# Eight of a layer's sixteen mixer gates made by a seven-product scheme at the mixer's front; FFN slices of 6, 8 and 8

## The chip, the cores and the metric

One core of one Trainium2 chip runs the whole decoder trunk in one launch. The time is the device time of one execution in microseconds, the median of several runs. All times inside an execution are microseconds from the start of its profiled span.

## The reference

Two layers over 512 tokens with 1024 channels, in float32. Only what the change touches is shown.

```python
for l in range(DEPTH):                                   # DEPTH = 2
    x = x + 0.5 * swiglu(rms_norm(x, ffn1_norm[l]), ffn1_w_up[l], ffn1_w_down[l])
    h = rms_norm(x, mix_norm[l])
    proj = h @ w_in[l]
    q, k, v, z, xbc, dt_raw, gate_sb, gate_ssm = jnp.split(proj, IN_SPLITS, axis=-1)
    y_sb  = stick_breaking_attention(q, k, v) @ w_branch_sb[l]        # 4 heads x 128
    y_ssm = mamba2_mixer(z, xbc, dt_raw, ...) @ w_branch_ssm[l]       # 24 heads x 64, 8 groups, state 128
    merged = jax.nn.sigmoid(gate_sb) * y_sb + jax.nn.sigmoid(gate_ssm) * y_ssm
    x = x + merged @ w_out[l]
    x = x + 0.5 * swiglu(rms_norm(x, ffn2_norm[l]), ffn2_w_up[l], ffn2_w_down[l])
return rms_norm(x, final_norm)
```

The two gates of a layer are 1024 channels each, so 8 blocks of 128 for each: sixteen gate blocks a layer. The hidden width of a feed-forward network (FFN) is 2816, or 22 blocks.

## The kernel before

Everything is held transposed, channels on the 128 partitions and the 512 tokens along the free axis; x is eight tiles of 128 x 512. A float32 product is made of three passes: weight and input are split into a high part (fp32r) and a low part, and `mm3` (lines 360 to 364) adds high x high, low x high and high x low. The weights come from one DRAM array, `wflat`, in units, in the order of `unit_order`. A plain unit is eight 128 x 128 blocks (512 KB): `fetch` loads it, `convert` makes its high part on ScalarE (line 327) and its low part on VectorE (line 329) two units ahead of its use. `dense` multiplies it, three matmuls of 512 columns a block.

A product X W with both sides cut in halves (tokens in two, input channels in two, output columns in two) needs eight products of halves. For pairs of FFN blocks (gate and up of blocks j and j+1) `pair_of_blocks` makes it from seven, named `SEVEN`: "11", "12", "s2", "s1", "s3", "s4", "22". Four use weights as stored, three use sums of weights (made by accumulating DMAs on GpSimd's queue, `onto`, line 289, or by VectorE, `add`, line 303). Three of the factors are differences of the input's halves, which `combine` makes (two ScalarE and four VectorE steps, then the split, lines 420 to 440) while the last products of the part before run. A product is 2 x 4 blocks of three matmuls of 256 columns.

The inputs h are x times the norm's gain; the root mean square `rs` is known only later (`norm_end`), so what is made before is scaled by `rs` afterwards. At the head of a seven-product FFN the pairs 0 and 2 come first as `leading`: "11" and "12" of both, which need no differences, then the rest.

A layer runs FFN 1, the mixer, FFN 2. An FFN runs in slices of its 22 blocks: gate and up of the slice's blocks, then eight `down` products over the slice. The slices are 8, 8 and 6 blocks, in FFN 2 of layer 0 they are 6, 8 and 8. The first six blocks of the first FFN are plain units.

The mixer (line 1376): first q, k, v and the attention; then the steps of `group_steps`: for each of four pairs p of state-space groups one z (four units), two b, two c and three x blocks, with gate units (`gs`, `gm`) put between them; then two `bsb` units (attention's branch product, four blocks each), then, for each of eight output blocks, the two `bssm` units (twelve blocks) with further `bsb` units between, and at last the `out` units. Twelve gates (`EARLY` = 6, times two) are squashed by a tanh (line 1351) and kept in DRAM (`gd`) until the merge, four stay in SBUF. In pair 0 there are four gate units, in pairs 1, 2 and 3 there are three, two and one, then two more, then the last four.

What is not a matmul of `dense` is written as generators that are advanced by `tick()`, once after each block of a unit (`by_tokens`, which makes z, ticks 24 times). A `yield n` waits n ticks. So the order of all instructions on each engine is fixed when the program is written, and the chip's engines run it in that order with semaphores between them. `conv_block` is the convolution behind each x, b and c unit, ending in transposes on TensorE that wait in `meet` for a common moment. `ssd_group` is one group: it starts when its inputs are there and the group before has ended, issues the matmuls of its first two and then of its last two chunks (lines 1243 and 1246), normalises (lines 1310 to 1320), and transposes the result (line 914) for `bssm`. `flush()` ticks until no generator is left, without matmuls of units; it stands behind the two `bsb` units.

Queues: SP issues the weight loads, the spills of gates and of x; GpSimd's queue the accumulating loads.

Of the kernel before, what the change touches and what calls it, by code (L numbers as in the profile page):

```python
# [12 lines left out]
ALU = mybir.AluOpType  # L13
# [38 lines left out]
G_D = G_ALOG + HEADS  # L52
NPAR = G_D + HEADS
EARLY = 6
MERGE_ORDER = tuple(range(EARLY, KB)) + tuple(range(EARLY))
OUT_ORDER = tuple(i // 2 + KB // 2 * (i % 2) for i in range(KB))
TAPS = KCONV + 1
# [3 lines left out]
def group_steps():  # L61

    gates = iter([(t, m) for m in range(EARLY) for t in ("gs", "gm")])
    for p in range(GROUPS // 2):
        a, b = 2 * p, 2 * p + 1
        if p == 0:
            steps = [("z", p), ("b", a), 1, ("c", a), ("x", 0), 1, ("x", 1), ("x", 2), 1, ("b", b), ("c", b), 1]
        else:  # L70
            steps = [("b", a), ("c", a), p < 2, ("x", 3 * p), ("x", 3 * p + 1), 1, ("z", p), ("x", 3 * p + 2),
                     ("b", b), p < 3, ("c", b), 0]
        for step in steps:
            if step in (0, 1):
                if step:
                    yield next(gates)
            else:
                yield step
    yield from gates
    for m in range(EARLY, KB):  # L80
        yield "gs", m
        yield "gm", m
# [20 lines left out]
def qkv_order():  # L103


    for h in range(SBH):
        yield from (("q", h), ("k", h))
        if h == SBH - 2:
            for u in range(NT):
                yield "v", u  # L110


def slices(layer, f):

    return ((0, 6), (6, 14), (14, 22)) if (layer, f) == (0, 2) else ((0, 8), (8, 16), (16, 22))


def pairs_from(layer, f):

    return {(0, 1): 6}.get((layer, f), 0)  # L120


def leading(layer, f):

    return [(layer, f, "pair", j, part) for j, parts in
            ((0, SEVEN[:2]), (2, SEVEN[:2]), (0, SEVEN[2:]), (2, SEVEN[2:])) for part in parts]


def unit_order(layer):

    def ffn(f):
        for s, (j0, j1) in enumerate(slices(layer, f)):
            start = j0
            if s == 0 and not pairs_from(layer, f):
                for key in leading(layer, f):
                    yield key, KB
                j0 = 4
            for j in range(j0, j1):
                if j < pairs_from(layer, f):
                    yield (layer, f, "gate", j), KB  # L140
                    yield (layer, f, "up", j), KB
                elif j % 2 == 0:
                    for part in SEVEN:
                        yield (layer, f, "pair", j, part), KB
            for m in OUT_ORDER:
                yield (layer, f, "down", s, m), j1 - start

    yield from ffn(1)
    for t, h in qkv_order():
        yield (layer, t, h), KB  # L150
    for kind, i in group_steps():
        if kind == "z":
            for u in range(NT):
                yield (layer, "z", i, u), 2 * 2 * GW // P + (i == 0)
        else:
            yield (layer, kind, i), KB
    for m in MERGE_ORDER[:2]:
        yield (layer, "bsb", m), SBH
    for i, m in enumerate(MERGE_ORDER):
        yield (layer, "bssm", m, 0), 6  # L160
        yield (layer, "bssm", m, 1), 6
        if i + 2 < KB:
            yield (layer, "bsb", MERGE_ORDER[i + 2]), SBH
    for m in OUT_ORDER:
        yield (layer, "out", m), KB
    yield from ffn(2)
# [12 lines left out]
class Builder:  # L179
# [433 lines left out]
        yield 2  # L613
        yield from self.split(parts, a)

    def pair_of_blocks(self, base, fp, two):

        nc, half, n = self.nc, SEQ // 2, KB // 2  # L620
        a, b = slice(0, half), slice(half, SEQ)
        diff = self.diff
        chain, ps2 = (self.t(self.pmm, [P, SEQ], "mm") for _ in range(2))
        ps3 = self.t(self.pa, [P, SEQ], "pa")

        def product(ps, part, rhs, cols, start):
            hi, lo = self.unit(*base, part)
            for j in range(2):
                for k in range(n):
                    ks = slice((j * n + k) * P, (j * n + k + 1) * P)  # L630
                    self.mm3(ps[:, j * half:(j + 1) * half], (hi[:, ks], lo[:, ks]),
                             [r[:, cols] for r in rhs[k]], start and j + k == 0, k == n - 1, skip_group_check=True)
                    if k % 2:
                        self.tick()

        def activate(g, c, cols):

            while self.rs is None:
                yield 1
            norm(nc.gpsimd if c is up1 and not lead else nc.vector, g, cols)  # L640
            yield (5 + 2 * base[-1] if lead else 4) if c is up1 else 1
            self.tables(False)
            nc.scalar.activation(g, g, AF.Silu)
            yield 1
            if c is up1:
                norm(nc.vector if lead else nc.gpsimd, g, cols)
                yield 1 if lead else 3
            while not c:
                yield 1
            r = self.t(fp, [P, SEQ], "a")  # L650
            nc.vector.scalar_tensor_tensor(r, c[0], -1.0, g, op0=ALU.mult, op1=ALU.mult)
            yield 1
            r = r.rearrange("p (j t) -> p j t", j=2)
            yield from self.split([t.rearrange("p (j t) -> p j t", j=2)[:, :, cols] for t in two], r)

        def normed_up(c):
            while self.rs is None:
                yield 1
            norm(nc.gpsimd, c, b)
            yield 3  # L660
            up2.append(c)

        def norm(eng, r, cols):
            r = r.rearrange("p (j t) -> p j t", j=2)
            eng.tensor_tensor(r, r, self.rs[:, cols].unsqueeze(1).to_broadcast([P, 2, half]), op=ALU.mult)  # L665

        up1, up2 = [], []
        lead = not pairs_from(*base[:2]) and base[-1] < 4
        g1, g2 = (self.t(fp, [P, SEQ], "g", bufs=4) for _ in range(2))
        product(chain, "11", self.h[:n], a, True)  # L670
        nc.scalar.copy(g1, chain)
        product(ps2, "12", self.h[n:], a, True)
        nc.vector.tensor_tensor(g1, g1, ps2, op=ALU.add)  # L673
        self.spawn(activate(g1, up1, a))
        yield
        while None in self.diff:
            self.tick()
        product(chain, "s2", diff[n:], b, False)
        nc.scalar.copy(g2, chain)
        product(ps3, "s1", diff[:n], a, True)  # L680
        c = self.t(fp, [P, SEQ], "c", bufs=2)
        nc.scalar.copy(c, ps3)
        product(chain, "s3", diff[:n], b, False)
        nc.vector.tensor_tensor(c, chain, c, op=ALU.add)
        self.spawn(normed_up(c))
        product(ps3, "s4", self.h[n:], b, False)
        nc.vector.tensor_tensor(g2, g2, ps3, op=ALU.add)
        self.spawn(activate(g2, up2, b))
        product(chain, "22", diff[n:], a, False)
        up1.append(chain)  # L690

    def down(self, pd, m, gain, last):
        x = self.x[m]
# [98 lines left out]
    def ffn(self, layer, f, gain, gain_next):  # L792
        tc = self.tc
        with tc.tile_pool(name=f"act{layer}{f}", bufs=8, reuse_waits="tile") as ap, \
                tc.tile_pool(name=f"ffn{layer}{f}", bufs=3, reuse_waits="tile") as fp:
            self.gated = {}
            for s, (j0, j1) in enumerate(slices(layer, f)):
# [41 lines left out]
                for i, m in enumerate(OUT_ORDER):  # L839
# [11 lines left out]
                    if last and i == 0:  # L851
                        self.norm_start()
                        self.xd = self.t(self.dr, [KB, P, SEQ], "xd") if f == 1 else None
                        if f == 1:
                            self.close_t()
                    self.spawn(self.down(ps, m, gain_next, last))


# [517 lines left out]
    def mixer(self, layer):  # L1376
        nc, tc = self.nc, self.tc
        self.y_sb, self.y_ssm = [], [None] * (DIN // P)
        gain = self.pars[layer][:, G_MIX:G_MIX + KB]
        self.open_norm(self.x, gain)  # L1380
        self.hx = []
        first = []
        order = list(qkv_order())
        for i in range(4):
            while i == 3 and self.scaled_blocks < KB // 2:
                self.tick()
            first.append(self.project(layer, *order[i], swap=i == 3, aside=i < 2))
        xd, self.xd = self.xd, None
        self.xpool.__exit__(None, None, None)
        with ExitStack() as mix:  # L1390
            enter = mix.enter_context
# [4 lines left out]
                tc.tile_pool(name=f"yt{layer}", bufs=24, side="right", reuse_waits="tile"))  # L1396
            gp = enter(tc.tile_pool(name=f"gates{layer}", bufs=2, reuse_waits="tile"))
            gates, self.gated = {}, {}

            self.gd = self.t(self.dr, [2 * EARLY, P, SEQ], "gd")  # L1400

            def open_gate(t, m):
                ps, _ = self.project(layer, t, m)
# [136 lines left out]
def lay_out(inputs):  # L1540
# [6 lines left out]
    for layer in range(DEPTH):  # L1547
# [2 lines left out]
        dt_w = np.zeros((DM, 64), np.float32)  # L1550
        dt_w[:, :HEADS] = w_in[:, OFF_DT:OFF_DT + HEADS]
        for key, n in unit_order(layer):
            kind = key[1] if key[1] not in (1, 2) else key[2]
            if kind == "pair":
                if key[-1] not in STORED:
                    continue
                r0, c0 = {"11": (0, 0), "12": (DM // 2, 0), "s1": (0, FFN), "22": (DM // 2, FFN)}[key[-1]]
                c0 += key[3] * P
                w = a[f"ffn{key[1]}_w_up"][layer][r0:r0 + DM // 2]
                blk = np.concatenate([w[:, c0:c0 + P], w[:, c0 + P:c0 + 2 * P]])  # L1560
            elif kind in ("gate", "up"):
                w = a[f"ffn{key[1]}_w_up"][layer]
# [76 lines left out]
```

## Time and profile before

| | us |
|---|---|
| median of 3 runs | 2551.49 (2551.28 to 2551.67) |
| profiled execution | 2551.46 |
| its span | 2549.7 |
| TensorE busy | 2539.5 |
| VectorE busy | 1731.6 |
| ScalarE busy | 1282.3 |
| GpSimd busy | 533.5 |

TensorE's busy time is the union of its instructions' intervals, whose ends are modelled, so it says that the queue never ran dry, not that the array was at its peak. How long one matmul holds the array is read from start to start of successive matmuls. In layer 0 the mixer's first projections start at about 350 us, the first group of the state-space part at 512, the merge at about 811; FFN 2 begins at about 942, FFN 1 of layer 1 at about 1274.

### The profile page before, as it was taken

Reading aid. Unit: us, or ns where it says so; the run is one execution under the profiler, and the core shown is the slowest. Engines: PE = TensorE matmul, PEld = TensorE weight load, DVE = VectorE, ACT = ScalarE, POOL = GpSimd, SP = SyncE. Lnnn points to the kernel's source line nnn. Section 1 sums busy time; section 2 is a strip of 40 time slices with the busy share of each in tenths; the row PEclk is TensorE's granted clock in tenths of the full one; section 3 lists DMA queues with packets and bytes.
Section 4 is the critical chain, followed back from the end, with each engine's and each line's share of the span. In section 5 each row is a group of like instructions: output and inputs, shape, how many; then the busy total and the mean of one; then the engine's idle time right before and its main releaser. Section 6 shows DMA issues by size and latency. Waiting matters only on the chain.

```text
span 2549.7 us, 38576 instructions
## 1 busy us (share of the span) xinstructions
PE 2539.5 (100%) x15248; PEld 2287.1 (90%) x15248; DVE 1731.6 (68%) x2240; ACT 1282.3 (50%) x2121; POOL 533.5 (21%) x642
## 2 busy tenths in 40 slices
PE   9999999999999999999999999999999999999998
PEld 8898988888898889989898989888988888999997
DVE  8576875666664477758895858756666644876766
ACT  6343556655554264435563535566655633643434
POOL 0131301043342001313121312011433310122220
PEclk9999999999999999999999999999999999999999
DMA  6454542232333475646564545323333335746562
GB/s 192 133 153 145 135 138 80 96 120 97 113 111 102 137 211 150 174 149 165 181 159 141 158 141 143 130 80 108 113 97 104 115 111 160 197 139 172 145 164 83
DMA packets 107684, 346.80 MB, mean 136 GB/s; under 512 B 12208, under 2 KB 15728, under 8 KB 107504
## 3 DMA queue, kind: packets, MB, share of 16 engines
q1 hardware_dynamic: 93536, 295.98, 35.1%
q0 software_dynamic: 13104, 47.72, 10.5%
q8 instruction: 120, 1.97, 0.3%
q10 hardware_dynamic: 864, 0.64, 0.1%
q14 instruction: 60, 0.49, 0.1%
HBM read 331.61 MB, written 12.68 MB: 135 GB/s over the span
## 4 chain that ended last, share of the span: by engine, by line
PE 98%; DVE 1%; issue 1%; DMA 0%; ACT 0%; POOL 0%; DVEq 0%; SPq 0%; POOLq 0%; ACTq 0%
PE mm L362 27%; PE mm L364 27%; PE mm L363 27%; PE pa L363 3%; PE pa L362 3%; PE pa L364 3%; PE pa L1243 2%; PE pa L1246 1%; PE pt L1225 1%; PE pt L914 1%; PE pt L1221 1%; DMA s<-in_wflat_dram 0%; PE pa L501 0%; PE pa L914 0%; PE pa L1031 0%
## 5 line engine op out<-in xcount | busy, mean ns | idle before, releaser
L327 ACT CAST whi<-wraw 128x1024 fp32r<-128x1024 f32 (+3 forms) x437 | 432.3, 989 | 692.4 <-PE mm L364 495.3
L329 DVE TENSOR_TENSOR wlo<-wraw,whi 128x1024 fp32r<-128x1024 f32 (+3 forms) x437 | 535.9, 1227 | 272.3 <-ACT whi L327 271.5
L362 PE MATMUL mm<-hhi,whi 128*128 128x512 f32 (+1 forms) x1536 | 533.5, 347 | 0.0
L364 PE MATMUL mm<-hlo,whi 128*128 128x512 f32 (+1 forms) x1536 | 526.8, 343 | 0.0
L363 PE MATMUL mm<-hhi,wlo 128*128 128x512 f32 (+1 forms) x1536 | 526.3, 343 | 0.0
L364 PEld LDWEIGHTS mm<-hlo,whi 128*128 128x128 f32 x1536 | 288.0, 187 | 35.4
L363 PEld LDWEIGHTS mm<-hhi,wlo 128*128 128x128 f32 x1536 | 288.6, 188 | 32.3
L362 PEld LDWEIGHTS mm<-hhi,whi 128*128 128x128 f32 x1536 | 288.5, 188 | 31.9
L362 PE MATMUL mm<-th,whi 128*128 128x256 f32 x984 | 275.4, 280 | 0.0
L363 PE MATMUL mm<-th,wlo 128*128 128x256 f32 x984 | 274.7, 279 | 0.5 <-DVE wlo L329 0.5
L364 PE MATMUL mm<-tl,whi 128*128 128x256 f32 x984 | 274.5, 279 | 0.0
L362 PE MATMUL mm<-act,whi 128*128 128x512 f32 (+1 forms) x710 | 273.9, 386 | 0.0
L363 PE MATMUL mm<-act,wlo 128*128 128x512 f32 (+1 forms) x710 | 273.7, 386 | 0.0
L364 PE MATMUL mm<-act,whi 128*128 128x512 f32 (+1 forms) x710 | 273.7, 385 | 0.0
L329 DVE TENSOR_TENSOR wlo<-s,whi 128x1024 fp32r<-128x1024 f32 x164 | 237.6, 1462 | 34.6 <-ACT whi L327 31.3
L665 POOL TENSOR_TENSOR g<-g,rs 128x512 f32<-128x512 f32 x70 | 148.9, 2127 | 506.9 <-DVE g L673 475.7
L289 POOL DMA_DIRECT2D s<-in_wflat_dram x91 | 79.7, 890 | 624.2 <-DMA s<-in_wflat_dram 509.9
L327 ACT CAST whi<-s 128x1024 fp32r<-128x1024 f32 x164 | 172.0, 1049 | 67.8 <-PE mm L364 48.8
L694 DVE SCALAR_TENSOR_TENSOR x<-mm,x 128x512 f32<-128x512 f32 x93 | 64.2, 690 | 206.6 <-PE mm L364 206.6
L364 PEld LDWEIGHTS mm<-tl,whi 128*128 128x128 f32 x984 | 184.9, 188 | 0.0
L362 PEld LDWEIGHTS mm<-th,whi 128*128 128x128 f32 x984 | 184.7, 188 | 0.2 <-issue 0.2
L363 PEld LDWEIGHTS mm<-th,wlo 128*128 128x128 f32 x984 | 184.1, 187 | 0.7 <-DVE wlo L329 0.7
(305 smaller groups left out, 5110.0 us busy)
## 6 DMA issues: line engine op xcount, KB each, us to landing
wraw<-in_wflat_dram SPq DMA_DIRECT2D x325, 512.0 KB, 3.7
s<-in_wflat_dram POOLq DMA_DIRECT2D x91, 512.0 KB, 7.4
s<-in_wflat_dram SPq DMA_DIRECT2D x85, 512.0 KB, 5.2
wraw<-in_wflat_dram SPq DMA_DIRECT2D x88, 384.0 KB, 3.1
cumb<-cum_d SPq DMA_DIRECT2D x16, 768.0 KB, 5.0
xd<-x SPq DMA_DIRECT2D x16, 256.0 KB, 2.4
wraw<-in_wflat_dram SPq DMA_DIRECT2D x16, 256.0 KB, 3.8
x<-xd SPq DMA_DIRECT2D x16, 256.0 KB, 5.5
```

What stands on the lines that cost most here:

```text
L289: self.nc.gpsimd.dma_start(raw, self.stored(key[:-1] + (part,)), accum_op=ALU.add)
L327: nc.scalar.copy(hi[:, :n], raw[:, :n])
L329: nc.vector.tensor_tensor(lo[:, :n], raw[:, :n], hi[:, :n].bitcast(F32), op=ALU.subtract)
L362: mm(ps, a[0], b[0], start=start, stop=False, **kw)
L363: mm(ps, a[1], b[0], start=False, stop=False, **kw)
L364: mm(ps, a[0], b[1], start=False, stop=stop, **kw)
L665: eng.tensor_tensor(r, r, self.rs[:, cols].unsqueeze(1).to_broadcast([P, 2, half]), op=ALU.mult)
L694: self.nc.vector.scalar_tensor_tensor(x, pd, 0.5, x, op0=ALU.mult, op1=ALU.add)
L914: self.nc.tensor.transpose(pt[:, cs], src[:, cs], self.ident)
L1221: nc.tensor.matmul(cb, bt[:, span(c)], ct[:, span(c)], start=True, stop=True)
L1225: nc.tensor.matmul(pu, btok[:, c, :], xws[c].rearrange("p h d -> p (h d)"), start=True, stop=True)
L1243: nc.tensor.matmul(near[:, at:at + HD], decs[c][:, i, :], xdts[c][:, i, :], start=True, stop=True)
```

## The change

Eight of the sixteen gates of a layer, blocks 2 to 5 of both kinds, leave `group_steps` and are made at the mixer's head, ahead of q, as two fours (block m and m+1 of both gates) of seven products each. `four_gates` takes the four results as they come, scales them by `rs` on VectorE, squashes them on ScalarE and writes each as two half blocks of 128 KB to `gd`. `pair_of_blocks` is cut in two: `seven` holds the products, and what becomes of the results is handed in. The differences of the input's halves are now made at the end of FFN 1 too, since the pool that holds them (`tpool`) stays open until the fours are done. Of the gate units among the group steps only the four of pair 0 and the last four stay. The slices are 6, 8 and 8 in all FFNs but the last, which keeps 8, 8 and 6.

```diff
+FRONT = 2
...
-    gates = iter([(t, m) for m in range(EARLY) for t in ("gs", "gm")])
+    gates = iter([(t, m) for m in range(FRONT) for t in ("gs", "gm")])
     for p in range(GROUPS // 2):
         a, b = 2 * p, 2 * p + 1
         if p == 0:
             steps = [("z", p), ("b", a), 1, ("c", a), ("x", 0), 1, ("x", 1), ("x", 2), 1, ("b", b), ("c", b), 1]
         else:
-            steps = [("b", a), ("c", a), p < 2, ("x", 3 * p), ("x", 3 * p + 1), 1, ("z", p), ("x", 3 * p + 2),
-                     ("b", b), p < 3, ("c", b), 0]
+            steps = [("b", a), ("c", a), ("x", 3 * p), ("x", 3 * p + 1), ("z", p), ("x", 3 * p + 2), ("b", b), ("c", b)]
...
-    yield from gates
     for m in range(EARLY, KB):
         yield "gs", m
         yield "gm", m
...
-    return ((0, 6), (6, 14), (14, 22)) if (layer, f) == (0, 2) else ((0, 8), (8, 16), (16, 22))
+    return ((0, 8), (8, 16), (16, 22)) if (layer, f) == (DEPTH - 1, 2) else ((0, 6), (6, 14), (14, 22))
...
     yield from ffn(1)
+    for key in leading(layer, 0):
+        yield key, KB
...
+    def normed_half(self, eng, out, r, cols):
+        r, out = (t.rearrange("p (j t) -> p j t", j=2) for t in (r, out))
+        eng.tensor_tensor(out, r, self.rs[:, cols].unsqueeze(1).to_broadcast([P, 2, SEQ // 2]), op=ALU.mult)
...
+    def four_gates(self, base, m, fp):
+        nc, half = self.nc, SEQ // 2
+        a, b = slice(0, half), slice(half, SEQ)
+        def squash(src, t, cols, scale):
+            while self.rs is None:
+                yield 1
+            r = self.t(fp, [P, SEQ], "c", bufs=2) if t and cols is a else src
+            self.normed_half(nc.vector, r, src, cols)
+            yield 2
+            self.tables(False)
+            nc.scalar.activation(r, r, AF.Tanh, scale=scale)
+            yield 4
+            for j in range(2):
+                nc.sync.dma_start(self.gd[2 * (m + j) + t][:, cols], r[:, j * half:(j + 1) * half])
+        def take(*how):
+            return lambda src: self.spawn(squash(src, *how))
+        return self.seven(base, fp, take(0, a, 0.5), take(1, b, -0.5), take(0, b, 0.5), take(1, a, -0.5))
...
                         self.norm_start()
                         self.xd = self.t(self.dr, [KB, P, SEQ], "xd") if f == 1 else None
-                        if f == 1:
-                            self.close_t()
...
         gain = self.pars[layer][:, G_MIX:G_MIX + KB]
+        self.gd = self.t(self.dr, [2 * EARLY, P, SEQ], "gd")
+        front = ExitStack()
+        fp = front.enter_context(tc.tile_pool(name=f"front{layer}", bufs=2, reuse_waits="tile"))
+        four = [self.four_gates((layer, 0, "pair", j), FRONT + j, fp) for j in range(0, EARLY - FRONT, 2)]
+        for part in four:
+            next(part)
+        for part in four:
+            for _ in part:
+                pass
+        self.close_t()
         self.open_norm(self.x, gain)
...
             first.append(self.project(layer, *order[i], swap=i == 3, aside=i < 2))
         xd, self.xd = self.xd, None
+        front.close()
         self.xpool.__exit__(None, None, None)
```

More of the change, by code (lines that the diff above doesn't have):

```diff
@@ L70, in group_steps @@
         else:
-            steps = [("b", a), ("c", a), p < 2, ("x", 3 * p), ("x", 3 * p + 1), 1, ("z", p), ("x", 3 * p + 2),
-                     ("b", b), p < 3, ("c", b), 0]
+            steps = [("b", a), ("c", a), ("x", 3 * p), ("x", 3 * p + 1), ("z", p), ("x", 3 * p + 2), ("b", b), ("c", b)]
         for step in steps:
[L74 to L78, printed above, removed]
-    yield from gates
+            yield next(gates) if step == 1 else step
     for m in range(EARLY, KB):
@@ L614, in up, with seven @@
         yield from self.split(parts, a)
-    def pair_of_blocks(self, base, fp, two):
+    def seven(self, base, fp, first, fourth, second, third):
         nc, half, n = self.nc, SEQ // 2, KB // 2
@@ L634, in product, with pair_of_blocks @@
                         self.tick()
+        g1, g2 = (self.t(fp, [P, SEQ], "g", bufs=4) for _ in range(2))
+        product(chain, "11", self.h[:n], a, True)
+        nc.scalar.copy(g1, chain)
+        product(ps2, "12", self.h[n:], a, True)
+        nc.vector.tensor_tensor(g1, g1, ps2, op=ALU.add)
+        first(g1)
+        yield
+        while None in self.diff:
+            self.tick()
+        product(chain, "s2", diff[n:], b, False)
+        nc.scalar.copy(g2, chain)
+        product(ps3, "s1", diff[:n], a, True)
+        c = self.t(fp, [P, SEQ], "c", bufs=2)
+        nc.scalar.copy(c, ps3)
+        product(chain, "s3", diff[:n], b, False)
+        nc.vector.tensor_tensor(c, chain, c, op=ALU.add)
+        fourth(c)
+        product(ps3, "s4", self.h[n:], b, False)
+        nc.vector.tensor_tensor(g2, g2, ps3, op=ALU.add)
+        second(g2)
+        product(chain, "22", diff[n:], a, False)
+        third(chain)
+    def normed_half(self, eng, out, r, cols):
+        r, out = (t.rearrange("p (j t) -> p j t", j=2) for t in (r, out))
+        eng.tensor_tensor(out, r, self.rs[:, cols].unsqueeze(1).to_broadcast([P, 2, SEQ // 2]), op=ALU.mult)
+    def pair_of_blocks(self, base, fp, two):
+        nc, half = self.nc, SEQ // 2
+        a, b = slice(0, half), slice(half, SEQ)
+        up1, up2 = [], []
+        lead = not pairs_from(*base[:2]) and base[-1] < 4
         def activate(g, c, cols):
@@ L639, in activate @@
                 yield 1
-            norm(nc.gpsimd if c is up1 and not lead else nc.vector, g, cols)
+            self.normed_half(nc.gpsimd if c is up1 and not lead else nc.vector, g, g, cols)
             yield (5 + 2 * base[-1] if lead else 4) if c is up1 else 1
@@ L645, in activate @@
             if c is up1:
-                norm(nc.vector if lead else nc.gpsimd, g, cols)
+                self.normed_half(nc.vector if lead else nc.gpsimd, g, g, cols)
                 yield 1 if lead else 3
@@ L658, in normed_up @@
                 yield 1
-            norm(nc.gpsimd, c, b)
+            self.normed_half(nc.gpsimd, c, c, b)
             yield 3
             up2.append(c)
[L663 to L690, printed above, removed]
+        return self.seven(base, fp, lambda g: self.spawn(activate(g, up1, a)), lambda c: self.spawn(normed_up(c)),
+                          lambda g: self.spawn(activate(g, up2, b)), up1.append)
@@ new lines, in four_gates @@
+    def four_gates(self, base, m, fp):
+        nc, half = self.nc, SEQ // 2
+        a, b = slice(0, half), slice(half, SEQ)
+        def squash(src, t, cols, scale):
[12 more added lines that the diff above has]
+        return self.seven(base, fp, take(0, a, 0.5), take(1, b, -0.5), take(0, b, 0.5), take(1, a, -0.5))
@@ L1398, in mixer @@
             gates, self.gated = {}, {}
-            self.gd = self.t(self.dr, [2 * EARLY, P, SEQ], "gd")
             def open_gate(t, m):
@@ L1552, in lay_out @@
         for key, n in unit_order(layer):
-            kind = key[1] if key[1] not in (1, 2) else key[2]
+            kind = key[1] if key[1] not in (0, 1, 2) else key[2]
             if kind == "pair":
@@ L1556, in lay_out @@
                     continue
-                r0, c0 = {"11": (0, 0), "12": (DM // 2, 0), "s1": (0, FFN), "22": (DM // 2, FFN)}[key[-1]]
-                c0 += key[3] * P
-                w = a[f"ffn{key[1]}_w_up"][layer][r0:r0 + DM // 2]
+                r0, half = {"11": (0, 0), "12": (DM // 2, 0), "s1": (0, 1), "22": (DM // 2, 1)}[key[-1]]
+                if key[1]:
+                    w, c0 = a[f"ffn{key[1]}_w_up"][layer], half * FFN
+                else:
+                    w, c0 = w_in, (OFF_GS, OFF_GM)[half] + FRONT * P
+                w, c0 = w[r0:r0 + DM // 2], c0 + key[3] * P
                 blk = np.concatenate([w[:, c0:c0 + P], w[:, c0 + P:c0 + 2 * P]])
```

## The prediction

> **What bounds the kernel now.** I read the page's busy shares and its chain first, then TensorE's own waits.
>
> ```profile
> span 2549.7 us, 38576 instructions
> PE 2539.5 (100%) x15248; PEld 2287.1 (90%) x15248; DVE 1731.6 (68%) x2240; ACT 1282.3 (50%) x2121; POOL 533.5 (21%) x642
> PE 98%; DVE 1%; issue 1%; DMA 0%; ACT 0%; POOL 0%; DVEq 0%; SPq 0%; POOLq 0%; ACTq 0%
> PE pt L1517 <- DVE ones L517: 1.1, 1, 1.1
> PE mm L363 <- DVE wlo L329: 0.5, 1, 0.5
> PE pt L742 <- ACT g L729: 0.2, 1, 0.2
> ```
>
> TensorE is 98% of the chain, and its three waits sum to 1.8 us. So the change can gain only matmul time, and it loses whatever wait it makes new. First the matmul's price: the timeline of TensorE, two rows of a plain unit (512 columns) and two of a seven-product part (256 columns).
>
> ```profile
> 798.38 0.39 PE L362 MATMUL mm<-hhi,whi 128*128 128x512 f32 x1
> 804.50 0.39 PE L362 MATMUL mm<-hhi,whi 128*128 128x512 f32 x1
> 1297.61 0.28 PE L362 MATMUL mm<-th,whi 128*128 128x256 f32 x1
> 1303.26 0.28 PE L362 MATMUL pa<-th,whi 128*128 128x256 f32 x1
> ```
>
> The first two starts lie 27 matmuls apart (three lines a step, nine steps): 6.12 / 27 = 0.227 us each. The other two lie 48 apart: 5.65 / 48 = 0.118 us. The durations printed (0.39, 0.28) overlap; only start to start counts.
>
> **The matmuls (gain).** A gate unit is 8 blocks x 3 passes = 24 matmuls of 512 columns, 24 x 0.227 = 5.45 us; a product is 2 x 4 x 3 = 24 of 256 columns, 24 x 0.118 = 2.83 us. Per layer eight units go (43.6 us) and fourteen products come (39.6 us): 4.0 us less. Two layers: **-7.9 us**. The change can bring no more than this and the 0.5 us wait above.
>
> **The front (new work at the head of the mixer).** Its nearest row is the head of FFN 1 in layer 1, which also follows an 8-block last slice, with the same two leading pairs, sums and differences.
>
> ```profile
> 1264.00:1304.00 40.00, 40.00 (x297) 38.08 (x296) 36.38 (x49) 27.06 (x39) 5.13 (x6) 1.00 0.60 152
> 1304.00:1310.00 6.00, 5.53 (x47) 5.32 (x46) 5.80 (x7) 4.37 (x7) 0.82 (x1) 1.00 0.93 208
> 1304.43 1.22 DVE L303 TENSOR_TENSOR s<-s,wraw 128x1024 f32<-128x1024 f32 x1
> 1305.56 1.22 DVE L329 TENSOR_TENSOR wlo<-s,whi 128x1024 fp32r<-128x1024 f32 x1
> 1306.70 0.68 DVE L456 TENSOR_TENSOR act<-a,act 128x512 fp32r<-128x512 f32 x1
> DMA to landing us min/median/max: 5.5/6.9/9.1
> ```
>
> The window columns are length, then busy time (and count) of PE, PEld, DVE, ACT, POOL, then clock, DMA share, GB/s. VectorE is 91% and then 97% busy there, and TensorE loses 0.5 us to it: such a head is just carried. Per layer the new front issues, where eight weight loads were: on SP six raw loads and five first halves of sums (512 KB each) and sixteen spills of 128 KB (eight of 256 KB before); on POOL's queue seven accumulating DMAs; on VectorE 14 low parts (1.22 us), two sums (1.22), six additions and eight scalings (about 0.7 each): 17.1 + 2.4 + 9.8 = 29 us in 39.6. Eight of the low parts were there before, later. Beside them come the four combines at the end of FFN 1; every other head has them too, that of the rows included. A pair costs VectorE about five 0.7 us steps behind its products (normalise twice, multiply, two low parts, less what POOL takes), a four costs four, with no low part to feed the next matmul. So I take half of the row's wait, **+0.25 us** a layer; ends 0 and 2.2, the latter if an accumulating DMA lands at the row's 9.1 us in place of 6.9. The spills wait for their tanh on SP in front of the weight prefetch, but are issued four ticks after it. The projections of q and k behind the front find the same scale_blocks work as before. A tanh table comes ahead of attention and the logarithm table is loaded again:
>
> ```profile
> 494.91 1.28 ACT L1095 ACT_TABLE_LOAD   x1
> ```
>
> That is two loads more a layer on ScalarE, half idle; the cover is the nine or so ticks (6 us) between a first score and the matmul that needs its logarithms. Cost 0; without cover 1.28 a layer.
>
> **The slices.** The same 22 blocks are multiplied. FFN 2 of layer 0 already runs 6, 8, 8, and the waits list has nothing of it. Cost 0.
>
> **The group stage (loss).** Side work moves by ticks: one per block of a unit, so 8 for a plain unit, 24 for a z, 4 for a bsb. A group holds the stage for 37 ticks when its inputs are there: its last two chunks' matmuls are issued at tick 26, the normalised y at 37, the transposes of it six later. The gates that go were filler in exactly this stage.
>
> ```profile
> 541.96 0.50 POOL L1201 TENSOR_TENSOR xw<-xs,sq 128x192 f32<-128x192 f32 x1
> 573.97 0.52 POOL L1201 TENSOR_TENSOR xw<-xs,sq 128x192 f32<-128x192 f32 x1
> 764.84 0.68 DVE L1318 TENSOR_TENSOR raw<-y,gny 128x512 f32<-128x512 f32 x1
> 771.28 0.47 ACT L1129 COPY btok<-pt 128x384 f32<-128x384 f32 x1
> 771.46 0.51 POOL L1201 TENSOR_TENSOR xw<-xs,sq 128x192 f32<-128x192 f32 x1 [7.27 <-ACT xs L1120]
> 692.00:720.00 28.00, 28.00 (x140) 23.68 (x139) 21.87 (x33) 17.39 (x36) 9.57 (x17) 1.00 0.27 85
> ```
>
> Groups 1 and 2 start 32.0 us apart: 37 ticks back to back. Group 7 starts (771.46) as its b in tokens is copied (771.28), 6.6 us after group 6 ended: late groups wait for TensorE, so taking filler out pulls them forward, until the 37 ticks bind. A pair without gates is 24 + 7 x 8 = 80 ticks against 2 x 37 = 74, so the middle holds; the densest stretch of convolutions now (692 to 720) has VectorE at 78% and no wait. The end does not hold. Count from the end of x block 10:
> - before: gate 8, z 32, x 40, b 48, c 56, six gates 104, two bsb 112. Group 7 starts at about 65, its last matmuls go out at 91, the transposes at 108: four ticks inside the cover.
> - after: z 24, x 32, b 40, c 48, four gates 80, two bsb 88. b's convolution takes 11 ticks to its transposes, these wait up to 7 more: start 59, last matmuls 85, y 96, transposes 102: fourteen ticks past the cover, in the flush ahead of the first bssm unit. TensorE, in order, stands.
>
> How long, from group 7's own chain (timeline, layer 0):
>
> ```profile
> 794.30 1.45 PE L1243 MATMUL pa<-xdt,dec 128*128 128x64 f32 x12
> 796.15 0.53 PE L362 MATMUL mm<-hhi,whi 128*128 128x512 f32 x1
> 796.49 0.62 DVE L1254 TENSOR_TENSOR t<-pa,sq 128x192 f32<-128x192 f32 x2
> 797.26 1.01 POOL L1258 TENSOR_TENSOR y<-y,t 128x384 f32<-128x384 f32 x1 [4.26 <-DVE t L1254]
> 798.35 1.16 POOL L1262 TENSOR_TENSOR y<-y,z 128x192 f32<-128x192 f32 x2
> 799.94 0.62 ACT L327 CAST whi<-wraw 128x512 fp32r<-128x512 f32 x1 [6.36 <-PE mm L364]
> 800.47 0.36 ACT L1269 ACTIVATE t<-y 128x192 f32<-128x192 f32 x1
> 801.63 1.02 POOL L1310 TENSOR_TENSOR gny<-ss,small 128x4 f32<-128x4 f32 x1
> 802.68 1.06 ACT L1320 ACTIVATE acc<-y,gny 128x64 f32<-128x64 f32 x4 [0.94 <-POOL gny L1310]
> 802.68 0.69 DVE L1318 TENSOR_TENSOR raw<-y,gny 128x512 f32<-128x512 f32 x1 [1.40 <-POOL gny L1310]
> ```
>
> From the first of these matmuls to the end of the normalised y: 803.37 - 794.30 = 9.07 us. In it the squares (800.47) wait 0.9 us behind a weight cast that itself waits for a later unit of TensorE; in the flush no cast is issued, so 8.2. TensorE's cover: its own two groups (796.15 - 794.30 = 1.85) and the three blocks left of the second bsb (9 x 0.227 = 2.04): 3.9. Stall 8.2 - 3.9 + 0.1 for the signal = **+4.4 us** a layer. The second transpose finds its tail ready (803.74, against 803.37 plus some 0.4). Ends: 0 if the transposes come in time after all, 5.3 if the 0.9 stays.
>
> **Sum.** Against the profiled execution's 2551.46 us (span 2549.7 and 1.8 around it; the median of the runs is 2551.49): 2551.46 - 7.9 + 2 x 4.4 + 2 x 0.25 = 2552.9; I say **2553.0**. Gain and loss cancel.
>
> **Rivals.**
> 1. *The tail is covered* (faster): group 7's inputs come some ten ticks earlier than counted, or its transposes stay behind bssm's first half. For it: TensorE has no such wait now. Against: b's last block ends 48 ticks before the cover does. 2551.46 - 7.9 + 0.5 = 2544.1; it decides once the stall is under 1.2 us a layer. 15%.
> 2. *The front stalls* (slower): sums late, VectorE at its limit. The row's 93% DMA share speaks for it, the missing low parts against. At 2.2 us a layer in place of 0.25: 2556.8; it decides from 2.1 us a layer. With the xd stores on SP beside it up to 4: 2560.4. 14%.
> 3. *The clock falls in the tail's wait.* The last windows of the trace:
>
> ```profile
> 2540.71 0.70 PE L742 MATMUL pt<-g,ones 128*128 128x256 f32 x2 [0.24 <-ACT g L729]
> 2544.00:2545.00 1.00, 0.00 (x0) 0.00 (x0) 1.00 (x4) 0.00 (x0) 0.00 (x0) 1.00 0.00 0
> 2545.00:2546.00 1.00, 0.00 (x0) 0.00 (x0) 1.00 (x4) 0.00 (x0) 0.00 (x0) 0.78 0.78 262
> ```
>
> TensorE ends at 2541.41 and the granted clock falls at about 2545.56 (0.78 over that microsecond, if it falls to a half): 4.15 us idle. The new stall is 4.4, just there. If half the clock then stays as long as the idle time took, that costs 2.1 us a fall: one fall 2555.0, two 2557.1. [...] Two falls: 9%; one stays in the forecast.
>
> **How the numbers follow.** Forecast 62%: 2550 to 2556.5, within 0.2% (5.1 us, about what a measurement of this kernel can tell from no change). Faster 15% (rival 1), slower 23% (rivals 2 and 3). The range leaves out the far half of rival 1 and of the slow cases: 2545 to 2559.
>
> **What would show it.** In the after trace: 256-column matmuls at 0.118 us and 7.9 us less of L362 to L364 start to start; a new wait of TensorE of about 4.4 us at L914 (transposes) before the first bssm unit, one per layer, released by VectorE's L1318; none over 0.5 us in the front; groups 2 to 5 starting some 32 us apart. The forecast is wrong if that wait is missing (2544), if a wait on a sum stands in the front, or if the clock column shows less than 1.00 there.

## The result: 2577.66 us, 26.2 us slower

| | before | after |
|---|---|---|
| median of 5 runs each, us | 2551.49 (2551.24 to 2551.67) | 2577.66 (2576.18 to 2578.35) |
| ratio, 95% interval | | 1.0103 (1.0088 to 1.0117) |
| span of the profiled execution | 2549.7 | 2576.0 |

The forecast was 2553.0, with a range up to 2559. The first lines of the page of after, and TensorE's list of waits (us in all, times, longest):

```profile
span 2576.0 us, 39402 instructions
PE 2545.2 (99%) x15536; PEld 2301.7 (89%) x15536; DVE 1795.5 (70%) x2332; ACT 1323.5 (51%) x2181; POOL 551.5 (21%) x656
PE mm L359 <- DVE cv L1115: 11.1, 6, 2.7
PE pa L939 <- DVE raw L1343: 7.5, 2, 3.7
PE pt L1551 <- DVE ones L514: 1.1, 1, 1.1
PE mm L359 <- DVE c L648: 0.8, 1, 0.8
PE pa L1054 <- DVE state L453: 0.6, 2, 0.3
PE mm L359 <- DVE z L1184: 0.3, 2, 0.2
```

The second wait (transposes on the normalised y, two times 3.7 us) was forecast. The first was not: 11.1 us in six waits of a unit's matmul on L1115, the taps of a convolution. And TensorE, which issues less matmul time than before, is busy 5.7 us longer: part of it ran at a lower clock (the mean granted clock is 0.995, in before 0.999).

**Where the time went.** Starts of the stages on TensorE in layer 0; layer 1 agrees within 0.1 us in the sum (12.55).

| stage, layer 0 | before | after | longer by |
|---|---|---|---|
| the new front | | 349.96 to 389.92 | 39.96 |
| q, k first | 349.95 to 383.77 | 389.92 to 423.33 | -0.41 |
| v to the end of the first z | 383.77 to 446.90 | 423.33 to 487.36 | 0.90 |
| group stage, up to the two bsb | 446.90 to 805.19 | 487.36 to 810.29 | -35.36 |
| the two bsb and the flush | 805.19 to 811.52 | 810.29 to 822.84 | 6.22 |
| bssm, up to out | 811.52 to 893.13 | 822.84 to 905.77 | 1.32 |
| sum | 543.18 | 555.81 | 12.63 |

The front costs what its products cost, 39.6 us and 0.36 more. The eight gates that left the group stage were 43.6 us, but the stage is only 35.4 shorter, and the tail is 6.2 longer. Of these 6.2 us, 1.9 are no loss: they are group 7's own matmuls (813.70 to 815.56), which before ran inside the group stage (794.30 to 796.15). So 8.2 + 1.9 = 10.1 us are lost inside the stage and 6.2 - 1.9 = 4.3 at the tail (the wait itself is 3.7), where 4.4 were forecast. The slices are neutral: the mixer starts at 349.95 and 349.96. Outside the mixers there is about 1 us in FFN 2 of layer 1, of which the wait on L648 is 0.8. In all 12.63 + 12.55 + 1.0 = 26.2.

**The lost time in the group stage.** The timeline of after where the first of these waits ends (pair 1, layer 0), VectorE's rows and TensorE's rows on both sides of the gap, and the row after the one of pair 3:

```profile
591.50 0.95 DVE L326 TENSOR_TENSOR wlo<-wraw,whi 128x768 fp32r<-128x768 f32 x1
592.36 0.75 DVE L1366 SCALAR_TENSOR_TENSOR yt<-pa,par,yt 128x512 fp32r<-128x512 f32 x1
593.02 0.74 DVE L1115 SCALAR_TENSOR_TENSOR cv<-mm,conv,cv 128x511 f32<-128x511 f32 x1
593.68 0.55 DVE L1260 TENSOR_TENSOR dec<-pt,dec 128x384 f32<-128x384 f32 x1
594.14 1.52 DVE L1115 SCALAR_TENSOR_TENSOR cv<-mm,conv,cv 128x510 f32<-128x510 f32 x2
592.78 0.34 PE L361 MATMUL mm<-wlo,hhi 128*128 128x384 f32 x1
595.81 0.41 PE L359 MATMUL mm<-whi,hhi 128*128 128x384 f32 x1 [2.69 <-DVE cv L1115]
...
742.23 0.41 PE L359 MATMUL mm<-whi,hhi 128*128 128x384 f32 x1 [1.99 <-DVE cv L1115]
```

z is made by tokens: its first of four weight units goes into four accumulators, one for each 128 tokens, opened one behind the other, six matmuls each. The pool of accumulators (`mm`) has four buffers. With three of them filled (18 matmuls, up to 592.78), the fourth is the bank of the x unit right ahead of z, and that is still being read by the three taps of its convolution on VectorE. VectorE comes to them late: in its rows a weight's low part, a y part and a decay stand ahead of the taps and between them. Before, a gate unit stood between that x and z; its 5.45 us were time for the taps. Six such places (three pairs, two layers) wait 2.69, 0.87 and 1.99 us a layer, 5.55 together.

**The clock.** Windows of 3.41 us of after, TensorE alone; columns are length, busy time (and count), granted clock, DMA share, GB/s:

```profile
593.38:596.79 3.41, 0.98 (x6) 1.00 0.43 154
596.79:600.20 3.41, 3.41 (x14) 0.50 0.02 5
740.15:743.56 3.41, 1.42 (x9) 1.00 0.38 138
743.56:746.97 3.41, 3.41 (x16) 0.50 0.00 0
818.66:822.07 3.41, 0.43 (x4) 1.00 0.75 272
822.07:825.48 3.41, 3.41 (x12) 0.50 0.00 0
1866.55:1869.96 3.41, 2.30 (x14) 1.00 0.22 56
1869.96:1873.38 3.42, 1.85 (x11) 1.00 0.25 97
2013.32:2016.73 3.41, 1.43 (x9) 1.00 0.70 235
2091.83:2095.24 3.41, 0.45 (x2) 1.00 0.98 319
2095.24:2098.65 3.41, 2.64 (x11) 0.50 0.24 94
2098.65:2102.07 3.42, 3.42 (x10) 0.50 0.26 67
```

After three of the waits in layer 0 the clock is granted at half for 3.41 us. I take half of that, 1.7 us, as the price of a fall, an estimate from the granted half (512-column matmuls start 0.43 us apart from 823.41 to 825.12, against 0.227 at whole clock; by that ratio it would be 1.6). The falls (596.79, 743.56, 822.07) lie 43.0 and 23.0 times 3.413 us apart, and that of layer 1 at 2095.24 lies 373.0 times from the last of them: in this trace they keep to one grid, while the waits ahead of them end 0.98, 1.33 and 0.43 us before the fall. The wait of 2.68 us that ends at 1871.53 has no fall; it lies across two windows of this grid and leaves 2.30 and 1.85 us of them busy. Layer 1 falls at 2016.73 (one window) and at 2095.24 (two). So by the estimate a layer pays about 5 us: three times 1.7 in layer 0, and 1.7 + 3.0 in layer 1 (half of the 2.64 and 3.42 us busy at half clock).

The loss of layer 0 is then 12.63 us and the 3.95 that the matmuls give, 16.6. Of it are waits at z 5.7 (L1115 and L1184), the transposes 3.7, clock 5.1, the front 0.4, a wait in the attention (L1054) 0.3. About 1.4 us a layer I can't put down to a row.

### The profile page after: what moved, and what is told of

Its sections match the earlier page's. It is cut to its first block, busy times and chain, and to the rows that moved or that the text cites. A ratio compares the mean times of both kernels' runs of the same rounds, so it can differ in the third digit from the quotient of the medians.

```text
span 2576.0 us, 39402 instructions
## 1 busy us (share of the span) xinstructions
PE 2545.2 (99%) x15536; PEld 2301.7 (89%) x15536; DVE 1795.5 (70%) x2332; ACT 1323.5 (51%) x2181; POOL 551.5 (21%) x656
## 4 chain that ended last, share of the span: by engine, by line
PE 92%; DVE 4%; ACT 2%; issue 1%; POOL 1%; DMA 0%; DVEq 0%; SPq 0%; POOLq 0%; ACTq 0%
PE mm L359 25%; PE mm L361 25%; PE mm L360 25%; PE pa L360 4%; PE pa L359 4%; PE pa L361 4%; PE pa L1268 2%; DVE wlo L326 1%; DVE cv L1115 1%; PE pa L1271 1%; ACT whi L324 1%; PE pt L939 1%; PE pt L1250 1%; PE pt L1246 0%; PE pa L498 0%
## 5 line engine op out<-in xcount | busy, mean ns | idle before, releaser
L359 PE MATMUL mm<-hhi,whi 128*128 128x512 f32 (+1 forms) x1472 | 501.0, 340 | 0.3 <-DVE z L1184 0.3
L361 PE MATMUL mm<-hlo,whi 128*128 128x512 f32 (+1 forms) x1472 | 494.8, 336 | 0.0
L360 PE MATMUL mm<-hhi,wlo 128*128 128x512 f32 (+1 forms) x1472 | 494.3, 336 | 0.0
L359 PE MATMUL mm<-th,whi 128*128 128x256 f32 x1080 | 302.2, 280 | 0.8 <-DVE c L648 0.8
L360 PE MATMUL mm<-th,wlo 128*128 128x256 f32 x1080 | 301.6, 279 | 0.2 <-DVE wlo L326 0.2
L361 PE MATMUL mm<-tl,whi 128*128 128x256 f32 x1080 | 301.3, 279 | 0.0
L326 DVE TENSOR_TENSOR wlo<-s,whi 128x1024 fp32r<-128x1024 f32 x180 | 257.2, 1441 | 35.3 <-ACT whi L324 31.7
L359 PEld LDWEIGHTS mm<-th,whi 128*128 128x128 f32 x1080 | 202.7, 188 | 1.0 <-issue 1.0
L361 PEld LDWEIGHTS mm<-tl,whi 128*128 128x128 f32 x1080 | 202.9, 188 | 0.0
L360 PEld LDWEIGHTS mm<-th,wlo 128*128 128x128 f32 x1080 | 202.2, 187 | 0.4 <-DVE wlo L326 0.4
```

Of the source, the lines that this page charges most:

```text
L326: nc.vector.tensor_tensor(lo[:, :n], raw[:, :n], hi[:, :n].bitcast(F32), op=ALU.subtract)
L359: mm(ps, a[0], b[0], start=start, stop=False, **kw)
L360: mm(ps, a[1], b[0], start=False, stop=False, **kw)
L361: mm(ps, a[0], b[1], start=False, stop=stop, **kw)
```

## The experiments

**Slices alone.** Before, with the new slices and nothing else.

```diff
-    return ((0, 6), (6, 14), (14, 22)) if (layer, f) == (0, 2) else ((0, 8), (8, 16), (16, 22))
+    return ((0, 8), (8, 16), (16, 22)) if (layer, f) == (DEPTH - 1, 2) else ((0, 6), (6, 14), (14, 22))
```

> The kernel before with the new slices alone (6, 8, 8 in all FFNs but the last). Theory: the slices move no wait, TensorE's work is the same: 2551.5, within 0.5 us. Rival: the shorter first slice or the longer last slice has a share in the 26 us: 2 us or more away from 2551.5, with a wait of TensorE at a down product.

One run: 2550.99, where before ran 2550.86 to 2552.51. By themselves the slices cost nothing that one run can tell.

**The bank set free early.** After, with the second x unit of pairs 1 to 3 copied out of its bank by ScalarE; the taps then read the copy. VectorE's work stays what it was.

```diff
         nc.scalar.activation(u, ps, AF.Identity, scale=tap[KCONV - 1], bias=tap[KCONV])
+        if kind == "x" and i >= 3 and i % 3 == 1:
+            nc.scalar.copy(r, ps)
+            ps = r
```

> The changed kernel, with one edit: the x unit right ahead of each z in pairs 1 to 3 is copied by ScalarE out of its PSUM bank at once, and VectorE's three taps read the copy. VectorE's work stays the same; ScalarE gets one 0.6 us copy for each of six units. Theory A (bank): z opens four accumulators at its start, the fourth is the bank of the x unit just before it, and TensorE waits until the taps have read it. Then TensorE's 11.1 us of waits on the taps go, and with them the three falls of the clock behind them (1.7 us each): 2577.7 - 11.1 - 5.1 = 2561.5. Theory B (VectorE is too slow for the denser stage): the waits stay or move to the next consumer, 8 us or more of them: 2573 to 2578.

2558.62 us, ratio to before 1.0027 (1.0018 to 1.0037), 19.0 less than after. TensorE's longest wait, a window of all engines (length, then busy time and count of PE, PEld, DVE, ACT, POOL, clock, DMA share, GB/s) around the z of pair 1, then the last two taps ahead of that z and the start of its fourth accumulator:

```profile
PE pa L939 <- DVE raw L1346: 7.5, 2, 3.7
590.00:596.00 6.00, 6.00 (x38) 5.96 (x37) 5.83 (x11) 2.60 (x5) 1.41 (x2) 1.00 0.27 91
594.53 1.53 DVE L1118 SCALAR_TENSOR_TENSOR cv<-raw,conv,cv 128x510 f32<-128x510 f32 x2
593.38 0.33 PE L359 MATMUL mm<-whi,hhi 128*128 128x384 f32 x1
```

All six waits on the taps are gone. From 450 to 805 us TensorE is busy 354.83 of 355 us at a granted clock of 1.00 (in after 349.29 at 0.99), and from 1720 to 2070 us 349.83 of 350 (in after 344.12). In the tail the clock still falls: its mean from 800 to 815 is 0.95. VectorE is no freer (5.83 of 6 us busy, 5.49 in the same window of after), and the taps end no earlier: at 596.06, in after at 595.66. But z opens its fourth accumulator at 593.38 and no longer waits for them. So what holds TensorE there is the bank, not VectorE's throughput, which was the rival. Six copies of 0.57 us on an engine that is half idle go with a time 19 us shorter: 11.1 of waits, 5.1 of clock (after's three falls in the group stages, by the estimate above), 2.8 not assigned.

**The order alone.** Before, with the gate moved behind z. Nothing of the work is changed.

```diff
-            steps = [("b", a), ("c", a), p < 2, ("x", 3 * p), ("x", 3 * p + 1), 1, ("z", p), ("x", 3 * p + 2),
+            steps = [("b", a), ("c", a), p < 2, ("x", 3 * p), ("x", 3 * p + 1), ("z", p), 1, ("x", 3 * p + 2),
```

> The kernel before, with one edit: the gate that stands between the second x unit and z in pairs 1 to 3 is put behind z. The same units, the same load on each engine. Theory A (bank): waits of TensorE on the taps at the third or fourth accumulator of z appear in the kernel before too, 0.5 to 2.7 us at each of six, with falls of the clock behind the longer ones: 2555 to 2568. Theory B (load): nothing changes, 2551.5 within 1 us.

2556.27 us, ratio 1.0017 (1.0008 to 1.0027): 4.6 us slower than before. The wait list's first line, TensorE's row of its first wait, and of before the three taps and the start of z's third accumulator:

```profile
PE mm L362 <- DVE cv L1090: 3.2, 2, 1.6
562.37 0.41 PE L362 MATMUL mm<-whi,hhi 128*128 128x384 f32 x1 [1.61 <-DVE cv L1090]
```

```profile
559.66 2.31 DVE L1090 SCALAR_TENSOR_TENSOR cv<-mm,conv,cv 128x511 f32<-128x511 f32 x3
564.79 0.33 PE L362 MATMUL mm<-whi,hhi 128*128 128x384 f32 x1
```

The order makes the wait without any new work: in before the same three taps ended at 561.97, and z came to their bank only at 564.79: with the gate in between, the round of the four buffers gives it to z's third accumulator. But only pair 1 of each layer waits, 1.6 us, and the mean granted clock is 0.999, as in before; the other four z do not, and 1.4 of the 4.6 us have no wait in the list. So the order alone gives 3.2 of after's 11.1 us. A as I had put it, with the order as the whole cause, claimed too much. For the rest the taps must come later in after than here; that its VectorE queue is denser ahead of them, since the gates are gone altogether, fits, but no run changes that by itself.

**A busy tail.** After, with 15 matmuls into an unused accumulator ahead of the flush; no result uses them. They fill the wait.

```diff
+                fill = self.t(self.ptr, [P, SEQ], "pt")
+                for _ in range(15):
+                    nc.tensor.matmul(fill, self.nones, self.y_sb[0][0], start=True, stop=True)
                 self.flush()
```

> The changed kernel, with 15 matmuls of 512 columns (3.4 us) into an unused PSUM tile between the second bsb unit and the flush, where TensorE waits 3.7 us for group 7's normalised y. Theory C (clock): TensorE's idle time there makes the granted clock fall, in layer 0 for one window of 3.4 us and in layer 1 for two. With the filler it doesn't fall there: the waits at the transposes shrink from 7.5 to under 1.5 us, and the time falls by 1.7 + 3.4 = 5 us to 2572.5, although no wait has been shortened. Rival: the low clock is not from this idle time, or costs nothing: 2577 to 2579.

2571.08 us, ratio 1.0077 (1.0062 to 1.0092): 6.6 less than after. TensorE's rows of the tail (layer 0), then the window behind it:

```profile
817.56 3.65 PE L1477 MATMUL pt<-ohi,nones 128*128 128x512 f32 x15
821.48 0.63 PE L939 MATMUL pa<-ident,raw 128*128 128x128 f32 x4 [0.27 <-DVE raw L1343]
820.50:826.00 5.50, 5.23 (x28) 4.17 (x27) 2.70 (x4) 2.84 (x7) 0.11 (x1) 1.00 0.17 56
```

The transposes come no earlier, as they wait for the group, but the granted clock behind them is 1.00 from 820.50 to 826.00. 6.6 us is what the falls behind the two tail waits cost in after by the estimate (1.7 + 3.0) and 1.9 more. The mean granted clock differs between executions: the profiled one is the slowest of the four (2573.35 us, clock 0.996), the two at 2570.2 and 2570.3 have 0.998, so one fall fewer would account for most of the 1.9. That is an estimate; only the profiled execution shows its windows. One of its falls, in layer 1:

```profile
1866.12:1869.53 3.41, 0.86 (x5) 1.00 0.45 154
1869.53:1872.94 3.41, 3.29 (x10) 0.50 0.00 0
```

This is the wait that had no fall in after: here 2.67 us long, ending at 1869.65, and it leaves 0.86 us busy in the 3.41 us ahead of the fall, where in after it left 2.30 and 1.85 us in two windows. So in these two traces the same wait went with a fall (1.7 us by the estimate) and without one. How much of the spread between runs comes from this isn't shown: the version with both losses mended, whose windows below show a clock of 1.00, spreads over 2.2 us too.

**The tail covered.** After, with the first halves of two bssm units put ahead of the flush (and the units' order to match).

```diff
+                halves = []
+                for m in MERGE_ORDER[:2]:
+                    halves.append(self.t(self.pmm, [P, SEQ], "mm"))
+                    self.dense(halves[-1], self.unit(layer, "bssm", m, 0), self.y_ssm, 0, 6, stop=False)
                 self.flush()
```

> The changed kernel, with one edit: the first halves of two bssm units (6 blocks each, they need only groups 0 to 3) go ahead of the flush, so that 36 matmuls (8.2 us) stand between the second bsb and group 7's transposes. Theory (the tail is short of cover by some four us, as predicted): the two waits of 3.7 us at the transposes go, and the low clock behind them, 7.5 + 5 = 12.5 us: 2577.7 - 12.5 = 2565; the waits on the taps at z stay as they are. Rival (the group's own chain is the bound, and stretches): the wait reappears at the second halves: 2573 or more.

2565.82 us, ratio 1.0054 (1.0039 to 1.0069), 11.8 less than after. Its wait list begins with the z waits, as long as in after, and has no line of the transposes:

```profile
PE mm L362 <- DVE cv L1118: 11.1, 6, 2.7
PE pt L1561 <- DVE ones L517: 1.1, 1, 1.1
```

The tail's whole price, waits and clock, is 11.8 us; the bank's is 19.0.

**Both mended.** The copy and the early halves together.

> The changed kernel, with the bank copy ahead of z and the two early halves of bssm. If the sum of theory is whole (matmuls -7.9, waits of z and tail gone, front and attention about +1.5), it is 2551.5 - 6.4 = 2545, faster than both. Rival (something of the 26 us is still unexplained, so that the seven-product gates cost what they save): 2550 or more.

2547.33 us (2546.68 to 2548.85), ratio 0.9983 (0.9974 to 0.9991): 4.5 us faster than before, and 30.3 less than after, where 19.0 + 11.8 is 30.8. It is 2.3 above the 2545 of the theory and below the rival's 2550. The wait list's first lines, the tail's rows of TensorE, and the whole state-space part of each layer in one window (TensorE alone):

```profile
PE pt L1564 <- DVE ones L517: 1.1, 1, 1.1
PE pa L1057 <- DVE state L456: 0.6, 2, 0.3
PE mm L362 <- DVE z L1190: 0.3, 2, 0.2
816.78 0.39 PE L364 MATMUL mm<-yt,whi 128*128 128x512 f32 x1
817.01 0.60 PE L942 MATMUL pa<-ident,raw 128*128 128x128 f32 x4
450.00:930.00 480.00, 479.83 (x2452) 1.00 0.36 116
1720.00:2190.00 470.00, 469.82 (x2402) 1.00 0.38 117
```

The transposes now follow a bssm matmul without a gap, and the granted clock is 1.00 in both windows. A layer's mixer takes 540.84 us against 543.18: 2.3 less, where the matmuls give 3.95. The front takes 0.36 of the difference, the attention some 0.5 (its wait of 0.3 included), the z wait on L1190 0.17; the other 0.6 has no row.

**The old slices with both mended.** The version above with the slices of before, to see whether the front needs the new ones.

```diff
-    return ((0, 8), (8, 16), (16, 22)) if (layer, f) == (DEPTH - 1, 2) else ((0, 6), (6, 14), (14, 22))
+    return ((0, 6), (6, 14), (14, 22)) if (layer, f) == (0, 2) else ((0, 8), (8, 16), (16, 22))
```

> The kernel with both edits, and the slices of before (8, 8, 6 in FFN 1), so that six-block down products stand ahead of the front. Theory (the slices give the sums and differences time): each down is 4.1 us in place of 5.4, so the sums are fetched some 5 us later against the front's need, and TensorE waits 1 to 5 us a layer in the front: 2547 to 2555. Rival (the slices make no odds): the same as with both edits, within 0.5 us.

2552.85 us, ratio 1.0006 (0.9997 to 1.0014): 5.5 us more than with the new slices, the whole gain. The first line of its wait list, and the front's first rows in layer 0:

```profile
PE mm L364 <- DVE hlo L547: 4.7, 4, 1.3
351.01 1.22 DVE L329 TENSOR_TENSOR wlo<-wraw,whi 128x1024 fp32r<-128x1024 f32 x1
352.15 0.75 DVE L547 SCALAR_TENSOR_TENSOR hlo<-x,par,hhi 128x512 fp32r<-128x512 f32 x1
352.95 0.39 PE L364 MATMUL mm<-hlo,whi 128*128 128x256 f32 x1 [1.20 <-DVE hlo L547]
```

I had expected late sums of weights, if anything; no wait on a sum is in the list. What waits are the first products, on low parts of the input h (L547), 4.7 us in four waits. VectorE makes such a part behind the low part of a weight: with only six blocks in FFN 1's last slice, a down unit lasts 18 x 0.227 = 4.1 us on TensorE instead of 5.45, and VectorE, with a combine and the norm beside them, has fallen behind by then. In layer 0 its rows follow one another without a gap from 349.62 to 357.70 us; with the new slices, in after, it stands idle for TensorE ahead of 350.17 (0.65 us). The size was in the expected span, its cause was another; that VectorE's lag is this cause is read from the rows, and no run tests it.

## Why the prediction was wrong, step by step

- **Matmuls, -7.9: right, but for 0.6 us a layer that have no row.** With both losses mended the mixers come out 2.3 us a layer shorter, and the rest of the missing part of the 3.95 is named above.
- **Front, +0.25 a layer between 0 and 2.2: right.** It measured 39.96 against 39.6, +0.36, with no wait of 0.5 us in it, and VectorE at 34.6 of 40 us:

```profile
350.00:390.00 40.00, 40.00 (x340) 39.91 (x339) 34.64 (x42) 28.28 (x38) 2.60 (x3) 1.00 0.68 182
```

- **Slices, 0: right in the sum, and for a reason that I had not given.** Alone they change nothing, but the front can't stand behind a slice of six blocks: that costs 2.8 us in layer 0 (its front takes 42.8) and 3.2 in layer 1. The row that I priced the front by did follow an eight-block slice; I had not asked what a six-block one does.
- **Table loads, 0: no wait on them is in the list** (after has 17 of 1.28 us, before 13).
- **"So the middle holds": the step that failed.** I counted the pace of the groups, 80 ticks against 74, and that part was right: the groups end 31 to 38 us apart and nothing waits for them in the middle (groups 2 to 5 start 31 to 36 us apart, where I said some 32). Then I costed the removed gates at nothing in the middle because VectorE is 78% busy there. But what the gate before z had covered was neither the groups nor VectorE's load: it was the time in which one bank is read. I priced the gates as matmuls and as ticks, and never asked which buffer the unit that moved up would take and who still reads it. That is 11.1 us of waits, and 19.0 with all that the copy took away.
- **Tail, +4.4 a layer between 0 and 5.3: right in place and cause, 3.7 in size.** The rows of group 7 in after:

```profile
813.70 1.45 PE L1268 MATMUL pa<-xdt,dec 128*128 128x64 f32 x12
818.38 0.36 ACT L1294 ACTIVATE t<-y 128x192 f32<-128x192 f32 x1 [4.33 <-POOL y L1287]
820.80 0.69 DVE L1343 TENSOR_TENSOR raw<-y,gny 128x512 f32<-128x512 f32 x1 [2.17 <-POOL gny L1335]
821.64 0.69 PE L939 MATMUL pa<-ident,raw 128*128 128x128 f32 x4 [3.73 <-DVE raw L1343]
```

  The squares wait for y and no more for a cast, as said; from the matmuls to the end of the normalised y it is 821.49 - 813.70 = 7.8 us where I took 8.2. The last matmuls go out five blocks into the two bsb, at the tick 85 that I had counted. No run stood behind the 0.1 us for the signal; in after the transposes start 0.15 us behind the end of the normalised y (821.49 to 821.64).
- **The clock, rival 3: one of its places was right, its threshold and its price were wrong.** I took 4.15 us idle as what a fall needs, from the end of before's trace, where TensorE does not come back. In after falls came behind waits of 3.73, 2.69 and 1.99 us, and each is worth 1.7 us (3.0 for the one of two windows) by the estimate above, where I took 2.1. I also said one or two falls in all, at 2557.1 at most; there were five, since the rival was tied to the tail alone. No run stood behind the 9% for two falls; both tail waits of after were followed by one. Nor did TensorE have to stand idle for as long as I took: in after, 3.41 us with 1.42 us of it busy (from 740.15) were followed by half clock.
- **Rivals 1 and 2 did not come.** The tail was not covered, and the front did not stall. (The border that I gave rival 1, a stall of 1.2 us a layer, gives 2546.5; the forecast's low end of 2550 is reached at 3.0. With 3.7 measured nothing hangs on it.)

The forecast's bounds were wrong in the same place: no case had a wait in the middle of the group stage, so the range ended 19 us below the result, and the chance of slower (0.23) came from the front and the clock.

## What to carry to other kernels

A unit that is moved or taken away is more than its matmul time: ask which buffers the next unit takes, who still reads them, and how long its neighbours had covered that reading. A unit that opens all buffers of a pool at once needs all of its readers done; a bank that three instructions of a busy engine read behind other work can be emptied by one copy on a less busy engine (here 0.57 us on ScalarE, and 19.0 us for six). And price each short wait of TensorE with the fall of the clock that may follow: here eight waits of 0.9 to 3.7 us (18.6 us) and the five falls behind them (some 10 us by the estimate) came to more than the 7.9 us that the change could ever gain.

## What the runs showed of the hardware that I had not expected

In the trace of after all falls of the granted clock lie on one grid: those at 596.79, 743.56, 822.07, 2016.73, 2095.24 and, at the end, 2569.69 are 43.0, 23.0, 350.0, 23.0 and 139.0 times 3.413 us apart. In its windows on this grid (TensorE's busy time is the profile's modelled one), those at whole clock with 1.43 us busy or less (0.43, 0.45, 0.98, 1.03, 1.42 and 1.43) were followed by half clock, and those with 1.85 us or more (1.85, 2.30, and 2.55 upward) were not. So in after a border would lie between 42% and 54% of a window; no run tests it by itself. The way back looks different there: the window from 2095.24, at half clock and 2.64 us busy (77%), was followed by another at half, while the five at half clock with all of their 3.41 us busy were followed by whole clock. A wait of 2.69 us (to 595.81) was followed by a fall and one of 2.68 us (to 1871.53) was not: the first left 0.98 us busy in one window, the second 2.30 and 1.85 us in two.
